# A two-layer hybrid attention trunk: the first eight loads of modulation weights shared between two issuing queues

## The chip, the cores and the metric

The kernel runs on one core of a Trainium2 chip. The core has a matrix engine (PE, with its weight loads listed apart as PEld), a vector engine (DVE), a scalar engine (ACT), GpSimd (POOL) and a sync engine (SP) that here only issues transfers. The metric is the device time of one execution in microseconds (us); lower is better. For the kernel before the change, three runs gave a median of 1925.78 us (1925.18 to 1926.59).

## What is computed

The input x has 512 rows and 2048 columns. Two layers are computed, all in float32; what matters here is how each layer begins:

```python
c_act = jax.nn.silu(c)                               # c: 2048 numbers
mod = c_act @ w_mod[l] + b_mod[l]                    # w_mod[l]: 2048 x 6144
shift, scale, gate = jnp.split(mod, 3, axis=-1)
h = x * (1.0 + scale[:, None]) + shift[:, None]
proj = h @ w_in                                      # layer 0: 2048 x 8192, then attention
...
x = layer_norm(DN_ALPHA * x + gate[:, None] * y, ln_g[l], ln_b[l])
```

Layer 0 is differential attention with 8 heads, layer 1 forgetting attention with 16 heads on keys and values projected once. Nothing of `h` exists before its columns of `shift` and `scale` do, and each of these needs a whole column of `w_mod`, 2048 rows deep.

## The kernel before, in words

Each float32 product is made of three products of rounded parts (high with high, high with low, low with high), so weights and activations are split: ACT casts the high part (`whi` at L125, `hh` at L694), DVE subtracts to get the low part (`wlo` at L132, `hl` at L709).

The start of the kernel makes `h` in the order of its 16 column blocks ("kt") while the first projections of two heads already run. The 16 blocks are grouped in nine sets, of which the first two hold one block each. For set 0, the weights of shift and scale are 2048 rows by 128 columns, twice: 2 MB. They come as eight loads of 256 KB, named **load 0 to load 7** below: loads 0 to 3 fill one tile (`sms_121` before, `sms_109` after the change), rows 0 to 1023, loads 4 to 7 the next tile (`sms_126`), rows 1024 to 2047; an even number is shift, an odd one scale, and each pair brings 512 rows. Loads 8 and on belong to set 1.

What is done with them: DVE multiplies 128 rows at a time by the column of `cact` that belongs to them and adds up in `sacc` (L616 for the first rows, L618 for the rest). Rows 6, 9, 10 and 13 (in blocks of 128) are left to PE (L646). Rows 12, 14 and 15 of the DVE's share, and row 13 of PE's, need loads 6 and 7. PE then sums `sacc` over the partitions (L660), DVE adds the bias and stores into `mcol` (L671), and only then can ACT make `hh` of block 0 (L694) and `htmp` (L701), from which DVE makes `hl` (L709). PE's projections of block 0 (L720) follow.

The order of each engine in this start is written out by hand as strings of letters (`ORDER_SP`, `ORDER_ACT`, `ORDER_PE`, `ORDER_DVE`): `L` is a load of modulation weights, `X` a load of x, `W` a load of projection weights (two transfers each), `a` a cast, `b` its subtraction, `F` a multiplication of PE that fills time and whose result nobody reads (L632), and so on. Before the strings are played, the kernel loads `c` and a part of the bias (L235, L236) on SP's queue and works out `cact = silu(c)` from it (L241 to L247). All loads of the start stand in SP's queue.

Every transfer counts its landing on one of eight completion counters, `DMAHW0` to `DMAHW7`, handed out in turn. A transfer that is given a counter for the second or third time is issued only after the transfer before it on that counter has landed; the issuing engine waits for it, in order, with all that stands behind.

Of the kernel before, what the change touches and what calls it, by code (L numbers as in the profile page):

```python
# [13 lines left out]
AF = mybir.ActivationFunctionType  # L14
ALU = mybir.AluOpType

P = 128
D = 2048
KT = D // P
# [125 lines left out]
def tile_yoco(  # L145
# [23 lines left out]
    nc = tc.nc  # L169
    V, S, PE, G = nc.vector, nc.scalar, nc.tensor, nc.gpsimd  # L170
# [25 lines left out]
    def tr_bank(name="tr"):  # L196
        return ps.tile([P, 512], F32, name=name, tag="tr", bufs=1)
# [14 lines left out]
    def corner(sc, q, k):  # L212
# [6 lines left out]
    ident = const.tile([P, P], F32, name="ident")  # L219
# [3 lines left out]
    mask = const.tile([P, 512], F32, name="mask")  # L223
# [7 lines left out]
    crow, brow = (  # L231
        kpool.tile([P, T], F32, name=name, tag="K")[:k, 0:P]
        for name, k in (("crow", KT), ("brow", 32))
    )
    nc.sync.dma_start(crow, c[0].rearrange("(a p) -> a p", p=P))  # L235
    nc.sync.dma_start(brow, b_mod[0, 0 : 2 * D].rearrange("(a p) -> a p", p=P))  # L236
    ccol = const.tile([P, KT], F32, name="ccol")
    pcol = const.tile([P, 38], F32, name="pcol")
    bcol = const.tile([P, 2, KT], F32, name="bcol")
    pt = tr_bank()  # L240
    PE.transpose(pt[:, 0:KT], crow, ident[0:KT, 0:KT])  # L241
    V.tensor_copy(ccol, pt[:, 0:KT])
    cact = const.tile([P, KT], F32, name="cact")
    tc.keep_in_program_order(S.activation(cact, ccol, AF.Exp, scale=-1.0))
    V.tensor_scalar(cact, cact, 1.0, None, op0=ALU.add)
    V.reciprocal(cact, cact)
    V.tensor_tensor(cact, cact, ccol, op=ALU.mult)  # L247
    pt = tr_bank()
    PE.transpose(pt[:, 0:32], brow, ident[0:32, 0:32])
    V.tensor_copy(bcol[:, 0, :], pt[:, 0:16])  # L250
    V.tensor_scalar(bcol[:, 1, :], pt[:, 16:32], 1.0, None, op0=ALU.add)
    gcol, bncol = pcol[:, 0:16], pcol[:, 16:32]

    neglam = const.tile([P, 1], F32, name="neglam")
# [232 lines left out]
    with tc.tile_pool(name="start", bufs=2, reuse_waits="tile") as sp, tc.manual_schedule(engines=MANUAL):  # L487
        mcol = const.tile([P, 2, KT], F32, name="mcol")

        fill = kpool.tile([P, T], F32R, name="fill", tag="K")  # L490
        S.copy(fill[:, 0:384], mask[:, 0:384])
        tiles = []
        for i, (k0, nk) in enumerate(sets):
            nr = 8 // nk
# [41 lines left out]
        cnt = dict.fromkeys("LXWpdmlbahicretoABCF", 0)  # L536
# [4 lines left out]
        def rows_read(n):  # L541

            i, k, nr = tiles[n]
            return all(
                ((i, r) in e_list[: cnt["e"]] if r in rows_pe[i] else (i, r) in d_list[: cnt["d"]]) for r in range(k, k + nr)
            )
# [12 lines left out]
        def op_L(j, queue=None):  # L559
            n, kq, step, v = loads[j]  # L560
            i, k, nr = tiles[n]
            k0, nk = sets[i]
            if n not in mtile:
                if n >= NBUF and not rows_read(n - NBUF):
                    return False
                mtile[n] = sp.tile([P, nr, 2, nk * P], F32, name="sms", tag="sms", bufs=NBUF)
            rows = w_mod[0, (k + kq) * P : (k + kq + step) * P, v * D + k0 * P : v * D + (k0 + nk) * P]
            (queue or nc.sync).dma_start(mtile[n][:, kq : kq + step, v, :], rows.rearrange("(k p) n -> p k n", p=P))  # L568
            return True
# [214 lines left out]
        def written(text):  # L784

            out, n = [], ""
            for ch in text:
                if ch.isdigit():
                    n += ch
                elif not ch.isspace():  # L790
                    out += (list("ABC") if ch == "g" else [ch]) * int(n or 1)
                    n = ""
            return out

        lists = [written(text) for text in (ORDER_SP, ORDER_ACT, ORDER_PE, ORDER_DVE)]
        kinds = ("LXWp", "ahicrK", "etoABCF", "dmlb")
        for text, kind in zip(lists, kinds):
            for ch in kind:
                if ch not in "KF":
                    text += [ch] * (total[ch] - text.count(ch) - (text.count("K") if ch == "L" else 0) - (lists[1].count("K") if ch == "L" else 0))  # L800
        at = [0] * 4
        while any(a < len(t) for a, t in zip(at, lists)):
            moved = False
# [1038 lines left out]
```

## Time and profile before

| what | value |
|---|---|
| median of three runs | 1925.78 us |
| the profiled execution, its own time | 1927.05 us |
| its span, first to last instruction | 1925.3 us |
| PE busy | 1910.1 us, 99% of the span |
| DVE, ACT busy | 1371.0 us, 732.9 us |
| mean granted clock of PE | 0.999 |
| moved by DMA | 382.22 MB, mean 199 GB/s |

Times below count from the first instruction of the profiled execution. In a row of the timeline stand the start, the time from the first start to the last end of the merged instructions, engine and line, what is written and read, how many, and in brackets the idle time of that engine before it and what ended it. "SPq" is SP's queue: the time in which it issues a transfer, not the one in which the data moves. An overlapped matmul is listed longer than the distance to the next one.

### The profile page before, as it was taken

Reading aid. Unit: us, or ns where it says so; the run is one execution under the profiler, and the core shown is the slowest. Engines: PE = TensorE matmul, PEld = TensorE weight load, DVE = VectorE, ACT = ScalarE, POOL = GpSimd, SP = SyncE. Lnnn points to the kernel's source line nnn. Section 1 sums busy time; section 2 is a strip of 40 time slices with the busy share of each in tenths; the row PEclk is TensorE's granted clock in tenths of the full one; section 3 lists DMA queues with packets and bytes.
Section 4 is the critical chain, followed back from the end, with each engine's and each line's share of the span. In section 5 each row is a group of like instructions: output and inputs, shape, how many; then the busy total and the mean of one; then the engine's idle time right before and its main releaser. Section 6 shows DMA issues by size and latency. Waiting matters only on the chain.

```text
span 1925.3 us, 25879 instructions
## 1 busy us (share of the span) xinstructions
PE 1910.1 (99%) x8921; PEld 1593.8 (83%) x8921; DVE 1371.0 (71%) x2617; ACT 732.9 (38%) x1266; POOL 2.3 (0%) x11
## 2 busy tenths in 40 slices
PE   8999999999999999999999999999999999999998
PEld 6888888888888888888888898888888888888887
DVE  7994588777776768667675477777566666686768
ACT  3656344333332344521272232224344344453122
POOL 0000000000000000000000000000000000000000
PEclk9999999999999999999999999999999999999999
DMA  9993566676767676476547586775345555555622
GB/s 339 385 339 91 158 187 197 209 239 189 235 197 225 203 225 182 123 241 221 184 164 251 181 297 209 250 266 162 112 147 159 158 150 162 154 153 168 226 93 110
DMA packets 352275, 382.22 MB, mean 199 GB/s; under 512 B 77912, under 2 KB 256244, under 8 KB 351376
## 3 DMA queue, kind: packets, MB, share of 16 engines
q1 hardware_dynamic: 349120, 376.25, 61.7%
q10 hardware_dynamic: 3024, 4.33, 0.6%
q8 instruction: 70, 1.15, 0.2%
q14 instruction: 61, 0.50, 0.1%
HBM read 348.68 MB, written 31.80 MB: 198 GB/s over the span
## 4 chain that ended last, share of the span: by engine, by line
PE 96%; DVE 2%; SPq 1%; DMA 1%; issue 0%; ACT 0%; DVEq 0%; ACTq 0%
PE acc L208 26%; PE acc L209 26%; PE acc L210 26%; PE acc L720 4%; PE sc L720 2%; PE sc L210 1%; PE sc L209 1%; PE sc L208 1%; PE o L208 1%; PE o L210 1%; PE o L209 1%; PE o L720 1%; SPq L568 1%; DMA sms<-in_w_mod_dram 0%; PE tr L686 0%
## 5 line engine op out<-in xcount | busy, mean ns | idle before, releaser
L113 ACT CAST whi<-wst 128x1024 fp32r<-128x1024 f32 (+2 forms) x298 | 303.4, 1018 | 616.4 <-PE acc L210 314.1
L114 DVE TENSOR_TENSOR wlo<-wst,whi 128x1024 fp32r<-128x1024 f32 (+2 forms) x298 | 351.4, 1180 | 248.5 <-ACT whi L113 222.7
L208 PE MATMUL acc<-hh,whi 128*128 128x512 f32 x1184 | 463.2, 391 | 0.0
L209 PE MATMUL acc<-hl,whi 128*128 128x512 f32 x1184 | 462.0, 390 | 0.0
L210 PE MATMUL acc<-hh,wlo 128*128 128x512 f32 x1184 | 460.3, 390 | 0.0
L208 PE MATMUL acc<-whi,hh 128*128 128x512 f32 (+1 forms) x1104 | 418.8, 380 | 0.0
L209 PE MATMUL acc<-wlo,hh 128*128 128x512 f32 (+1 forms) x1104 | 417.0, 378 | 0.0
L210 PE MATMUL acc<-whi,hl 128*128 128x512 f32 (+1 forms) x1104 | 416.5, 378 | 0.0
L433 DVE SCALAR_TENSOR_TENSOR macc<-ms,cact,macc 128x512 f32<-128x512 f32 x307 | 228.9, 746 | 61.2 <-DMA ms<-in_w_mod_dram 44.4
L210 PEld LDWEIGHTS acc<-hh,wlo 128*128 128x128 f32 x1184 | 222.4, 188 | 47.0
L208 PEld LDWEIGHTS acc<-hh,whi 128*128 128x128 f32 x1184 | 222.5, 188 | 44.1 <-DVE sgb L1509 0.8
L209 PEld LDWEIGHTS acc<-hl,whi 128*128 128x128 f32 x1184 | 222.6, 188 | 42.2
L210 PEld LDWEIGHTS acc<-whi,hl 128*128 128x128 f32 x1104 | 207.4, 188 | 38.6
L208 PEld LDWEIGHTS acc<-whi,hh 128*128 128x128 f32 x1104 | 207.4, 188 | 37.5 <-DVE ztmp L1241 0.6
L209 PEld LDWEIGHTS acc<-wlo,hh 128*128 128x128 f32 x1104 | 207.5, 188 | 35.6
L618 DVE SCALAR_TENSOR_TENSOR sacc<-sms,cact,sacc 128x512 f32<-128x512 f32 (+1 forms) x128 | 89.9, 702 | 6.2 <-DMA sms<-in_w_mod_dram 2.9
L904 ACT ACTIVATE e<-e,mn 128x128 f32<-128x128 f32 (+3 forms) x64 | 36.0, 563 | 111.1 <-DVE mn L900 104.5
L1559 ACT ACTIVATE eb<-eb,mnb 128x128 f32<-128x128 f32 (+1 forms) x64 | 35.9, 561 | 73.8 <-DVE mnb L1556 73.5
L720 PE MATMUL acc<-wlo,hh 128*128 128x512 f32 x128 | 49.9, 399 | 0.6 <-DVE wlo L132 0.6
L720 PE MATMUL acc<-whi,hl 128*128 128x512 f32 x128 | 49.4, 394 | 0.0
L720 PE MATMUL acc<-whi,hh 128*128 128x512 f32 x128 | 49.2, 393 | 0.0
L132 DVE TENSOR_TENSOR wlo<-wst,whi 128x768 fp32r<-128x768 f32 (+1 forms) x32 | 34.8, 1088 | 17.3 <-ACT whi L125 16.2
(336 smaller groups left out, 2095.6 us busy)
## 6 DMA issues: line engine op xcount, KB each, us to landing
wst<-in_a_w_in_dram SPq DMA_DIRECT2D x240, 256.0 KB
ms<-in_w_mod_dram SPq DMA_DIRECT2D x136, 256.0 KB
ms<-in_kv_w_mod_dram SPq DMA_DIRECT2D x64, 512.0 KB
wst<-in_b_w_in_dram SPq DMA_DIRECT2D x128, 256.0 KB
sms<-in_w_mod_dram SPq DMA_DIRECT2D x56, 512.0 KB
wst<-in_kv_w_dram SPq DMA_DIRECT2D x56, 512.0 KB
ms<-in_w_mod_dram SPq DMA_DIRECT2D x32, 512.0 KB
wst<-in_a_w_out_dram SPq DMA_DIRECT2D x32, 512.0 KB
```

The costliest lines, as they stand in the source:

```text
L113: self.nc.scalar.copy(hi[:, :, :w], st[:, :, :w])
L114: self.nc.vector.tensor_tensor(lo[:, :, :w], st[:, :, :w], hi[:, :, :w].bitcast(F32), op=ALU.subtract)
L132: self.nc.vector.tensor_tensor(lo[:, :, :w], st[:, :, :w], hi[:, :, :w].bitcast(F32), op=ALU.subtract)
L208: PE.matmul(dst, lhs[0], rhs[0], start=start, stop=False, skip_group_check=True)
L209: PE.matmul(dst, lhs[0], rhs[1], start=False, stop=False, skip_group_check=True)
L210: PE.matmul(dst, lhs[1], rhs[0], start=False, stop=stop, skip_group_check=True)
L433: ins = V.scalar_tensor_tensor(acc, w, cact[:, kt : kt + 1], acc, op0=ALU.mult, op1=ALU.add)
L568: (queue or nc.sync).dma_start(mtile[n][:, kq : kq + step, v, :], rows.rearrange("(k p) n -> p k n", p=P))
L618: V.scalar_tensor_tensor(acc, w, sc, acc, op0=ALU.mult, op1=ALU.add)
L720: PE.matmul(bank[n, bk], l, r, start=start, stop=stop, skip_group_check=True)
L904: S.activation(e[:, :w], e[:, :w], AF.Exp, bias=mn, scale=-1.0, accum_out=rs)
L1559: S.activation(e[:, :w], e[:, :w], AF.Exp, bias=mn, scale=-1.0, accum_out=rs)
```

## The change

The loads of `c` and of the bias, the work on `cact`, and the cast that makes the operand of PE's fillers move from the head of the kernel to the place just before the strings are played, and the first eight `L` are taken out of the strings and issued by hand, four of them on ACT's queue:

```diff
+        def first_loads(*queues):
+            for queue in queues:
+                op_L(cnt["L"], queue)
+                cnt["L"] += 1
+                del lists[0][lists[0].index("L")]
+
+        nc.sync.dma_start(crow, c[0].rearrange("(a p) -> a p", p=P))
+        nc.sync.dma_start(brow, b_mod[0, 0 : 2 * D].rearrange("(a p) -> a p", p=P))
+        first_loads(nc.scalar, nc.sync, nc.scalar, nc.sync)
+        pt = tr_bank()
+        PE.transpose(pt[:, 0:KT], crow, ident[0:KT, 0:KT])
+        V.tensor_copy(ccol, pt[:, 0:KT])
+        S.activation(cact, ccol, AF.Exp, scale=-1.0)
...
+        S.copy(fill[:, 0:384], mask[:, 0:384])
+        first_loads(nc.sync, nc.scalar, nc.sync, nc.scalar)
```

So ACT issues loads 0, 2, 5 and 7, SP loads 1, 3, 4 and 6. Outside these places and the first six rows of DVE (the two that make `bcol` now stand behind the three that make `cact`) every engine has the same instructions in the same order as before.

The first rows of ACT before; a DMA row is a transfer that the engine issues, "waits" names the counters that it must see first:

```order
L244 ACT_TABLE_LOAD
L244 ACTIVATE cact_101<-ccol_95 128x16 [waits DVE_49]
L491 CAST fill_119<-mask_86 128x384 [waits Pool_49]
L125 CAST whi_153<-wst_136 128x2x384 [waits DMAHW6_49,DMAHW5_49]
L694 ACTIVATE hh_214<-px_168,mcol_118 128x512 [waits DVE_49]
```

The first rows of ACT in the change:

```order
L554 DMA sms_109<-in_w_mod_dram 128x4x128 x2
L799 ACT_TABLE_LOAD
L799 ACTIVATE cact_96<-ccol_93 128x16 [waits DVE_49]
L807 CAST fill_106<-mask_86 128x384 [waits Pool_49]
L554 DMA sms_126<-in_w_mod_dram 128x4x128 [waits DMAHW0_49]
L554 DMA sms_126<-in_w_mod_dram 128x4x128 [waits DMAHW2_49]
L125 CAST whi_153<-wst_136 128x2x384 [waits DMAHW4_49,DMAHW3_49]
L680 ACTIVATE hh_214<-px_168,mcol_105 128x512 [waits DVE_49]
```

Loads 0 and 2 now stand ahead of ACT's table load and wait for nothing; loads 5 and 7 stand ahead of its first cast and wait for a counter each.

The first rows of SP before (the first four loads, then loads 4 and 5, then 6 and 7 each with a counter, x, and set 1 with the first projection weights):

```order
L235 DMA crow_91<-in_c_dram 16x128
L236 DMA brow_92<-in_b_mod_dram 32x128
L568 DMA sms_121<-in_w_mod_dram 128x4x128 x4
L568 DMA sms_126<-in_w_mod_dram 128x4x128 x2
L568 DMA sms_126<-in_w_mod_dram 128x4x128 [waits DMAHW0_49]
L568 DMA sms_126<-in_w_mod_dram 128x4x128 [waits DMAHW1_49]
L578 DMA xt_131<-in_x_dram 128x4x128 [waits DMAHW2_49]
L568 DMA sms_133<-in_w_mod_dram 128x4x128 [waits DMAHW3_49]
L568 DMA sms_133<-in_w_mod_dram 128x4x128 [waits DMAHW4_49]
L63 DMA wst_136<-in_a_w_in_dram 128x2x256 [waits DMAHW5_49]
```

The first rows of SP in the change (loads 1 and 3, then 4 and 6, then x and what follows):

```order
L793 DMA crow_91<-in_c_dram 16x128
L794 DMA brow_92<-in_b_mod_dram 32x128
L554 DMA sms_109<-in_w_mod_dram 128x4x128 x2
L554 DMA sms_126<-in_w_mod_dram 128x4x128 x2
L564 DMA xt_131<-in_x_dram 128x4x128 [waits DMAHW0_49]
L554 DMA sms_133<-in_w_mod_dram 128x4x128 [waits DMAHW1_49]
L554 DMA sms_133<-in_w_mod_dram 128x4x128 [waits DMAHW2_49]
L63 DMA wst_136<-in_a_w_in_dram 128x2x256 [waits DMAHW3_49]
L63 DMA wst_136<-in_a_w_in_dram 128x2x128 [waits DMAHW4_49]
L554 DMA sms_133<-in_w_mod_dram 128x4x128 [waits DMAHW5_49]
L63 DMA wst_140<-in_a_w_in_dram 128x2x256 [waits DMAHW6_49]
L63 DMA wst_140<-in_a_w_in_dram 128x2x256 [waits DMAHW7_49]
```

SP issues four transfers fewer ahead of x. Counter by counter, the built program hands out: 0 to load 0, then x, then load 5; 1 to `c`, load 8, load 11; 2 to the bias, load 9, load 7; 3 to load 2 and 4 to load 1, then each to half of the first projection weights. Each landing adds 16. The wait of load 5 is for 32 on counter 0, which is the landing of x; that of load 7 is for 32 on counter 2, which is the landing of load 9.

More of the change, by code (lines that the diff above doesn't have):

```diff
@@ L234, in tile_yoco @@
     )
-    nc.sync.dma_start(crow, c[0].rearrange("(a p) -> a p", p=P))
-    nc.sync.dma_start(brow, b_mod[0, 0 : 2 * D].rearrange("(a p) -> a p", p=P))
     ccol = const.tile([P, KT], F32, name="ccol")
@@ L239, in tile_yoco @@
     bcol = const.tile([P, 2, KT], F32, name="bcol")
-    pt = tr_bank()
-    PE.transpose(pt[:, 0:KT], crow, ident[0:KT, 0:KT])
-    V.tensor_copy(ccol, pt[:, 0:KT])
     cact = const.tile([P, KT], F32, name="cact")
[L244 to L251, printed above, removed]
     gcol, bncol = pcol[:, 0:16], pcol[:, 16:32]
@@ L490, in tile_yoco @@
         fill = kpool.tile([P, T], F32R, name="fill", tag="K")
-        S.copy(fill[:, 0:384], mask[:, 0:384])
         tiles = []
@@ L800, in tile_yoco @@
                     text += [ch] * (total[ch] - text.count(ch) - (text.count("K") if ch == "L" else 0) - (lists[1].count("K") if ch == "L" else 0))
+        def first_loads(*queues):
[10 more added lines that the diff above has]
+        S.activation(cact, ccol, AF.Exp, scale=-1.0)
+        V.tensor_scalar(cact, cact, 1.0, None, op0=ALU.add)
+        V.reciprocal(cact, cact)
+        V.tensor_tensor(cact, cact, ccol, op=ALU.mult)
+        pt = tr_bank()
+        PE.transpose(pt[:, 0:32], brow, ident[0:32, 0:32])
+        V.tensor_copy(bcol[:, 0, :], pt[:, 0:16])
+        V.tensor_scalar(bcol[:, 1, :], pt[:, 16:32], 1.0, None, op0=ALU.add)
+        S.copy(fill[:, 0:384], mask[:, 0:384])
+        first_loads(nc.sync, nc.scalar, nc.sync, nc.scalar)
         at = [0] * 4
```

## The prediction

> **What bounds the kernel now.** I read the page's first line and its table of engines, then the chain of work that ended last.
>
> ```profile
> span 1925.3 us, 25879 instructions
> PE 1910.1 (99%) x8921; PEld 1593.8 (83%) x8921; DVE 1371.0 (71%) x2617; ACT 732.9 (38%) x1266; POOL 2.3 (0%) x11
> PE 96%; DVE 2%; SPq 1%; DMA 1%; issue 0%; ACT 0%; DVEq 0%; ACTq 0%
> ```
>
> PE carries 96% of the chain. The rest, some 4%, lies mostly ahead of PE's steady work. A change to the first eight loads can therefore move the end only by moving the moment at which PE stops waiting. So the next view is PE's timeline over the first 60 us, for the rows where PE waited after its first projection.
>
> ```profile
> 15.97 0.73 PE L720 MATMUL sc<-hh,whi 128*128 128x512 f32 x2
> 17.37 0.73 PE L720 MATMUL sc<-hl,whi 128*128 128x512 f32 x2 [0.43 <-DVE hl L709]
> 25.39 0.73 PE L720 MATMUL sc<-hh,whi 128*128 128x512 f32 x2 [0.87 <-ACT hh L694]
> 36.03 0.74 PE L720 MATMUL acc<-wlo,hh 128*128 128x512 f32 x2 [0.60 <-DVE wlo L132]
> 60.00:120.00 60.00, 60.00 (x291) 49.97 (x290) 55.20 (x77) 37.35 (x56) 0.00 (x0) 1.00 1.05 364
> ```
>
> Projections begin at 15.97; PE then waits three times, 0.43 + 0.87 + 0.60 = 1.90 us in all, and from 36.03 on it does not wait again in this stage (the last row is the window from 60 to 120 us, whose second number is PE's busy time: all of it). A delay that reaches PE before 36.03 is passed to the end, less what these waits can swallow. What the start itself waits for:
>
> ```profile
> 0.73 0.40 SPq L235 DMA_DIRECT2D crow<-in_c_dram  x1
> 1.64 5.58 SPq L568 DMA_DIRECT2D sms<-in_w_mod_dram  x8
> 7.26 0.69 SPq L578 DMA_DIRECT2D xt<-in_x_dram  x1
> 2.58 0.26 PE L241 MATMUL tr<-ident,crow 16*128 16x16 f32 x1 [2.58 <-DMA crow<-in_c_dram]
> 5.30 0.35 DVE L616 TENSOR_SCALAR sacc<-sms,cact 128x256 f32<-128x256 f32 x1 [1.01 <-DMA sms<-in_w_mod_dram]
> 11.10 1.52 DVE L618 SCALAR_TENSOR_TENSOR sacc<-sms,cact,sacc 128x256 f32<-128x256 f32 x3 [0.48 <-DMA sms<-in_w_mod_dram]
> 13.00 0.85 PE L660 MATMUL tr<-ones,sacc 128*128 128x1 f32 x4
> 13.37 0.35 DVE L616 TENSOR_SCALAR sacc<-sms,cact 128x256 f32<-128x256 f32 x1 [0.74 <-DMA sms<-in_w_mod_dram]
> 13.72 2.38 PE L632 MATMUL fb<-fill 128*128 128x384 f32 x7
> 13.89 0.16 DVE L671 TENSOR_TENSOR mcol<-tr,bcol 128x2 f32<-128x2 f32 x1 [0.17 <-PE tr L660]
> 14.41 0.83 ACT L125 CAST whi<-wst 128x768 fp32r<-128x768 f32 x1 [10.71 <-DMA wst<-in_a_w_in_dram]
> 15.14 0.77 ACT L694 ACTIVATE hh<-px,mcol 128x512 fp32r<-128x512 f32 x1
> ```
>
> DVE's three waits are landings: loads 0 and 1 by 5.30, loads 6 and 7 by 11.10, loads 8 and 9 by 13.37. ACT's is the first projection weights, by 14.41. From loads 6 and 7 the path runs on through L618, L660, L671 and ACT's L694; PE meanwhile runs its seven fillers, which end when `hh` is there. The start is a queue of transfers, so I also read how full the DMA engines are (last number GB/s, the one before it their busy share).
>
> ```profile
> 0.00:4.00 4.00, 0.72 (x3) 0.54 (x4) 0.69 (x5) 1.90 (x3) 1.60 (x9) 1.00 0.27 77
> 4.50:6.50 2.00, 0.00 (x0) 0.00 (x0) 1.13 (x3) 0.00 (x0) 0.00 (x0) 1.00 0.84 224
> 10.00:12.00 2.00, 2.00 (x10) 2.00 (x11) 1.44 (x4) 0.00 (x0) 0.00 (x0) 1.00 1.14 342
> ```
>
> At 342 GB/s a load of 262 kB takes 0.77 us; x, load 8 and load 9, the three that land from 11.10 to 13.37, give 2.27 / 3 = 0.76. The engines are full by 10 us and were not from 4.5 to 6.5.
>
> **What the change removes and adds.** *Issue moved forward.* The first load was issued at 1.64, behind `c` and the bias; on ACT's queue it can be issued at 0.73, 0.91 us earlier. Loads 5 and 7 also leave the queue ahead of x, so x is the seventh large transfer and not the ninth: 2 x 0.76 = 1.52 earlier. Before, x landed one transfer behind load 7: 11.10 + 0.76 = 11.86. In the change: 11.86 - 0.91 - 1.52 = **9.43**. Load 9 follows two transfers later, at 10.95.
>
> *Waits added.* By the rows of ACT and their counters, load 5 is issued only when x has landed and load 7 only when load 9 has landed. That turns round the order in which data is needed: set 1's load 9 comes ahead of set 0's load 7. Load 7 is issued at about 10.95 + 0.10 = 11.05. Its own way has two terms: `c`, a load of 8 kB, was issued at 0.73 and released PE at 2.58, so 1.85 us pass apart from the moving of data, and the data takes 0.77 at full rate. 11.05 + 1.85 + 0.77 = **13.67**, where load 7 had landed by 11.10. Call the difference s = 13.67 - 11.10 = 2.57 us.
>
> No row here shows a load of ACT's queue beside a full queue of SP's, so its price is bounded from both sides. At the least, the transfers run without the slack of 4.5 to 6.5: at 224 GB/s, 2 x (1 - 224/342) = 0.69 us could come back and s be 1.88. At the most it waits like a load behind SP's own backlog: x was issued at 7.26 and landed at 11.86, 4.60 later; 11.05 + 4.60 = 15.65, s = 4.55. I take 2.57, near the lower end, because ACT's own queue is empty then and the row of `c` is the one of an empty queue.
>
> [...]
>
> *What s does further on.* The last three rows of DVE's set 0 start at 13.67, and L660, L671 follow as before: `mcol` at 13.89 + 2.57 = 16.46. The fillers of PE stand behind L660 in PE's order, so PE's first projection is at 15.97 + 2.57 = 18.54. DVE's low part comes from this row, with an idle time before it that a later start removes:
>
> ```profile
> 16.62 0.69 DVE L709 TENSOR_TENSOR hl<-htmp,hh 128x512 fp32r<-128x512 f32 x1 [0.26 <-ACT htmp L701]
> 18.83 4.12 DVE L618 SCALAR_TENSOR_TENSOR sacc<-sms,cact,sacc 128x256 f32<-128x256 f32 x8
> 23.65 0.16 DVE L671 TENSOR_TENSOR mcol<-tr,bcol 128x2 f32<-128x2 f32 x1
> 31.72 3.11 DVE L618 SCALAR_TENSOR_TENSOR sacc<-sms,cact,sacc 128x512 f32<-128x512 f32 x4 [1.22 <-DMA sms<-in_w_mod_dram]
> ```
>
> So `hl` is late by 2.57 - 0.26 = 2.31. From there through `mcol` of set 1 at 23.65 DVE has next to no idle time, so PE's row at 25.39 is late by 2.31 too. Up to 36.03 two things swallow: PE's own wait of 0.60, and DVE's 1.22 for a landing at 31.72, which is no longer waited for as the transfers are early. The larger remainder counts: PE 2.31 - 0.60 = 1.71, DVE 2.31 - 1.22 = 1.09. **The sum is +1.71 us**, or s - 0.86.
>
> *Edits at nothing.* The table load moves behind two issues of some 0.45 us each, to about 1.6, and its activation waits for `ccol` anyway:
>
> ```profile
> 0.73 1.28 ACT L244 ACT_TABLE_LOAD   x1 [0.73 <-PEq L1829]
> 3.08 0.21 ACT L244 ACTIVATE cact<-ccol 128x16 f32<-128x16 f32 x1 [1.07 <-DVE ccol L242]
> ```
>
> 1.07 us idle covers 0.9 of delay; beyond that DVE's 1.01 at 5.30 covers. `c` and the bias now travel beside loads 0 and 2. If they are held up by both, 2 x 0.77 = 1.54, DVE starts set 0 that much later, at 6.8; it has nine rows of some 0.5 us there before its last three, 4.6 us, and until 13.67 to do them, so nothing comes of it. Two `bcol` rows of 0.17 us behind `cact` lie in the same idle time. On ACT, the first cast stands behind the issue of load 7 (over by about 11.6); its weights, before at 14.41, come 0.91 + 1.52 earlier, near 12, and `hh` waits for `mcol` at 16.46, which covers it by over 3 us. If load 9 were late by more than that, the cast and with it `hh`, `htmp` and every later cast would be.
>
> **Rivals.** *The change does what it says: early loads, early start.* Then the wait of ACT costs nothing and the 0.91 us (with the 0.69 of slack, 1.60) arrive at PE: the start at 15.06 to 14.37. Later waits take part of it, since transfers are early by the same: -0.9, up to -1.6. For it: 77 GB/s in the first 4 us, room that a second queue can fill. Against: it needs load 7 by 10.2, and x alone, the seventh transfer, cannot land before 0.73 + 1.85 + 7 x 0.77 = 7.97, load 9 not before 9.5, load 7 not before 9.5 + 2.7 = 12.2 (s = 1.1, +0.2).
>
> *Load 7 behind SP's backlog.* One mechanism: the DMA engines serve ACT's late loads as if they stood at the end of SP's queue. Place: load 7, 4.60 us from issue to landing; price s = 4.55, +3.7 us. [...] For it: the engines' share of 1.14 at 10 to 12 us, no gap to slip into. Against: ACT's queue is empty.
>
> *Washed out.* If transfers gain more by 25 us than I count, or s is the 1.1 above, PE is at 36.03 within 0.3 us of before: 0. For: only s beyond 0.86 arrives. Against: DVE has next to nothing to give between 16.6 and 30.5 us:
>
> ```profile
> 16.60:30.50 13.90, 12.60 (x64) 9.98 (x63) 13.28 (x22) 4.64 (x7) 0.00 (x0) 1.00 1.11 373
> ```
>
> Its fourth number is DVE's busy time, 13.28 of 13.90, and the rest is in gaps between instructions.
>
> **How the numbers follow.** The profiled execution took 1927.05 us with a span of 1925.3, so 1.75 lie around it; it stands 1.27 above the median of the runs, 1925.78. Against its own time the forecast is 1927.05 + 1.7 = 1928.8, and against the median 1925.78 + 1.7 = **1927.5**. Chances: forecast 0.60 (+0.6 to +2.8 by the bounds and the half rate), backlog 0.14 (+3.7, 1929.5), washed out 0.14 (1925.8), early start 0.12 (-0.9 to -1.6, 1924.2 to 1924.9). The three runs before differ by 1.4 us, so I allow 0.3 beyond the backlog's time: 1924.6 to 1929.8.
>
> A measurement of this kernel can tell about 0.2% from no change, which is 3.9 us. Of the cases only the far end of the backlog gets there: slower 0.05. A gain of 3.9 us would need more than the start holds: 0.01. Within 0.2%: 0.94.
>
> **What would show it.** Right: ACT's third and fourth transfers issued near 9.5 and 11; DVE idle for some 2 to 3 us ahead of its last three rows of set 0, which start near 13.7; L671 near 16.5; PE's first projection near 18.5; no wait at the row that stood at 36.03, and that row 1.7 us later. Wrong: ACT's late issues before 8 us, or those three DVE rows before 12, for the early start; the three rows after 15, for the backlog. Also wrong would be a PE that waits again after 36 us, where I count nothing: the weights of the next steps then come later than PE needs them.

## The result, and the profile after

The changed kernel takes 1931.30 us (median of nine runs, 1930.53 to 1932.17); the kernel before took 1926.22 in the nine runs beside them (1925.18 to 1927.72). The ratio is 1.0025, interval 1.0016 to 1.0034: **slower by 5.1 us, 0.26%**. The forecast was +1.7, and its range ended at 1929.8. The profiled execution took 1931.31 with a span of 1929.5.

The page of the changed kernel, with the same three lines as shown of before:

```profile
span 1929.5 us, 25877 instructions
PE 1910.2 (99%) x8921; PEld 1594.0 (83%) x8921; DVE 1370.4 (71%) x2617; ACT 732.6 (38%) x1266; POOL 2.3 (0%) x11
PE 97%; DVE 1%; DMA 1%; SPq 0%; issue 0%; ACT 0%; ACTq 0%
```

PE is busy for 1910.2 us, where it was 1910.1. So the span's 4.2 us more are time in which PE has nothing to do. (The profiled execution of before, 1927.05, stood 0.83 above the median of the nine runs, that of the change at its own; 4.26 + 0.83 = 5.09, the difference of the medians.)

The chain of waits of the changed kernel over the start, in order of time (start, us, what; a DMA row runs from the issue to the landing, "..." stands for rows left out, and rows named issue, of 0.04 at most, are left out without it):

```profile
0.73 2.99 DMA sms<-in_w_mod_dram
3.76 1.55 SPq L564
5.35 0.77 SPq L554
6.17 4.39 DMA sms<-in_w_mod_dram
10.58 5.82 DMA sms<-in_w_mod_dram
16.45 0.58 PE tr L632 x2
...
19.08 2.45 PE fb L618 x7
21.53 0.85 PE sc L706 x2
...
24.53 0.46 PE acc L706 x2
```

This view shows where the time goes. Load 0 lands at 3.72; that lets SP issue x (3.76, L564), then loads 8 and 9. Load 9 is issued at 6.17 and lands at 10.56, which lets ACT issue load 7 at 10.58, and load 7 is 5.82 us on its way. PE goes on 0.05 after it has landed. The row at 19.08 is PE's seven fillers: `hh` is there from 20.09 on (19.31 + 0.78 on ACT), but the fillers stand ahead of the first projection in PE's order and hold it until 21.33; no run left them out. Two rows are for later: two projections of one size take 0.85 at 21.53 and 0.46 at 24.53.

The timeline of the changed kernel (start, us, engine, line, operation, in brackets the idle time before and what ended it):

```profile
6.12 0.35 DVE L602 TENSOR_SCALAR sacc<-sms,cact 128x256 f32<-128x256 f32 x1 [1.47 <-DMA sms<-in_w_mod_dram]
9.10 1.86 ACTq L554 DMA_DIRECT2D sms<-in_w_mod_dram  x2
11.73 0.83 ACT L125 CAST whi<-wst 128x768 fp32r<-128x768 f32 x1 [7.55 <-DMA wst<-in_a_w_in_dram]
14.44 2.59 PE L632 MATMUL tr<-cact,sms 128*128 128x1 f32 x10 [6.29 <-DMA sms<-in_w_mod_dram]
14.48 1.01 DVE L604 SCALAR_TENSOR_TENSOR sacc<-sms,cact,sacc 128x256 f32<-128x256 f32 x2 [4.88 <-DMA sms<-in_w_mod_dram]
16.48 1.53 DVE L604 SCALAR_TENSOR_TENSOR sacc<-sms,cact,sacc 128x256 f32<-128x256 f32 x3 [1.00 <-DMA sms<-in_w_mod_dram]
19.12 0.16 DVE L657 TENSOR_TENSOR mcol<-tr,bcol 128x2 f32<-128x2 f32 x1 [0.84 <-PE tr L646]
19.31 0.78 ACT L680 ACTIVATE hh<-px,mcol 128x512 fp32r<-128x512 f32 x1 [6.75 <-DVE mcol L657]
21.33 1.05 PE L706 MATMUL sc<-hh,whi 128*128 128x512 f32 x2
28.48 0.50 PE L646 MATMUL tr<-ones,sacc 128*128 128x1 f32 x4
29.02 0.16 DVE L657 TENSOR_TENSOR mcol<-tr,bcol 128x2 f32<-128x2 f32 x1 [0.87 <-PE tr L646]
30.77 0.73 PE L706 MATMUL sc<-hh,whi 128*128 128x512 f32 x2 [0.87 <-ACT hh L680]
40.65 0.61 PE L706 MATMUL acc<-wlo,hh 128*128 128x512 f32 x2
```

DVE's last three rows of set 0 stand at 16.48, where they were at 11.10: **s is 5.38**. Row by row the lateness of PE is: first projection 15.97 to 21.33, +5.36; second block 25.39 to 30.77, +5.38; the row that stood at 36.03 with a wait of 0.60 is at 40.65 with none, +4.62; the span, +4.2. The casts were in time (11.73, long before `mcol` at 19.12).

Three windows of the changed kernel (from:to, length, busy PE, PEld, DVE, ACT, POOL, granted clock, DMA share, GB/s):

```profile
11.50:16.50 5.00, 1.92 (x9) 1.84 (x9) 0.99 (x3) 0.83 (x1) 0.00 (x0) 1.00 1.14 353
21.30:23.60 2.30, 2.30 (x7) 1.78 (x7) 2.30 (x4) 0.40 (x1) 0.00 (x0) 1.00 1.10 382
60.00:120.00 60.00, 60.00 (x295) 50.03 (x295) 55.04 (x77) 37.87 (x58) 0.00 (x0) 1.00 0.99 334
```

While PE and DVE wait for load 7, the DMA engines run at 353 GB/s. Most of what they move is other data: by the counters further below, what was issued before load 7. From 60 us on PE is busy all the time, as before.

### The profile page after: what moved, and what is told of

It is laid out like the page before. It is cut to its first block, busy times and chain, and to the rows that moved or that the text cites. A ratio compares the mean times of both kernels' runs of the same rounds, so it can differ in the third digit from the quotient of the medians.

```text
span 1929.5 us, 25877 instructions
## 1 busy us (share of the span) xinstructions
PE 1910.2 (99%) x8921; PEld 1594.0 (83%) x8921; DVE 1370.4 (71%) x2617; ACT 732.6 (38%) x1266; POOL 2.3 (0%) x11
## 3 DMA queue, kind: packets, MB, share of 16 engines
q10 hardware_dynamic: 5136, 5.38, 0.8%
## 4 chain that ended last, share of the span: by engine, by line
PE 97%; DVE 1%; DMA 1%; SPq 0%; issue 0%; ACT 0%; ACTq 0%
PE acc L208 26%; PE acc L209 26%; PE acc L210 26%; PE acc L706 5%; PE sc L706 2%; PE sc L210 1%; PE sc L209 1%; PE sc L208 1%; PE o L208 1%; PE o L210 1%; PE o L706 1%; PE o L209 1%; DMA sms<-in_w_mod_dram 1%; PE tr L646 0%; PE tr L672 0%; DMA ms<-in_w_mod_dram 0%
## 5 line engine op out<-in xcount | busy, mean ns | idle before, releaser
L113 ACT CAST whi<-wst 128x1024 fp32r<-128x1024 f32 (+2 forms) x298 | 303.4, 1018 | 618.4 <-PE acc L210 300.9
L604 DVE SCALAR_TENSOR_TENSOR sacc<-sms,cact,sacc 128x512 f32<-128x512 f32 (+1 forms) x128 | 89.9, 703 | 10.2 <-DMA sms<-in_w_mod_dram 6.8
```

Source lines behind the costliest of these rows:

```text
L113: self.nc.scalar.copy(hi[:, :, :w], st[:, :, :w])
L604: V.scalar_tensor_tensor(acc, w, sc, acc, op0=ALU.mult, op1=ALU.add)
```

## The experiments

**Which half loses: two kernels.** `first_loads` shares the first four loads, then the next four. One kernel keeps the early sharing only (ACT has loads 0 and 2, nothing later), the other the late sharing only (ACT has loads 5 and 7).

Early half alone:

```diff
         S.copy(fill[:, 0:384], mask[:, 0:384])
-        first_loads(nc.sync, nc.scalar, nc.sync, nc.scalar)
+        first_loads(nc.sync, nc.sync, nc.sync, nc.sync)
```

> Only the early half of the change: ACT issues loads 0 and 2 ahead of its table load, loads 5 and 7 stay on SP's queue in their places. Theory (the loss comes from loads 5 and 7 being issued only after x and load 9 have landed): the loss is gone; eight loads land by about 9.8 us, the last three DVE rows of set 0 start near 9.9 (11.10 before), PE's first projection near 14.8 (15.97 before), time -0.3 to -1.2 us against before. Rival (two issuing queues cost by themselves, in c arriving later or in shared DMA engines): +1 us or more, with DVE's last three rows at 11 or later.

Measured: 1925.43 us (11 runs, 1924.67 to 1926.80) against 1926.58 of before (31 runs); ratio 0.9994, interval 0.9985 to 1.0003. The timeline of this kernel:

```profile
6.20 5.69 DVE L604 SCALAR_TENSOR_TENSOR sacc<-sms,cact,sacc 128x256 f32<-128x256 f32 x11
15.21 1.05 PE L706 MATMUL sc<-hh,whi 128*128 128x512 f32 x2
16.49 1.05 PE L706 MATMUL sc<-hl,whi 128*128 128x512 f32 x2
25.11 0.73 PE L706 MATMUL sc<-hh,whi 128*128 128x512 f32 x2 [0.87 <-ACT hh L680]
```

DVE's eleven rows of L604 run without a wait: load 7 is no longer the last thing. PE starts 0.76 earlier than before (15.21 against 15.97), of which 0.28 is left at the second block (25.11 against 25.39), since its first projections run at a slow rate (1.05 a pair; more on this below). Before, PE then had the wait of 0.60 at 36.03, which is gone here: matched row by row, PE is 1.0 ahead there and 1.5 from 60 us on. Nothing of the loss is in this half.

Late half alone:

```diff
         nc.sync.dma_start(brow, b_mod[0, 0 : 2 * D].rearrange("(a p) -> a p", p=P))
-        first_loads(nc.scalar, nc.sync, nc.scalar, nc.sync)
+        first_loads(nc.sync, nc.sync, nc.sync, nc.sync)
```

> Only the late half of the change: loads 0 to 4 and 6 on SP, loads 5 and 7 on ACT behind the cast of the filler, so that they wait for the landing of load 4 and of x. Theory with in-order service (a late load lands behind all that SP issued before it, 5.3 to 5.8 us from issue to landing as in the change): load 7 issued near 10.3, lands near 15.9, time +3.5 to +5 us. Rival (ACT's queue gets a share of its own, 2.6 to 3.4 us from issue to landing): lands near 13.3, time +1.5 to +2.5 us.

Measured: 1931.39 us (8 runs, 1930.51 to 1932.47); ratio 1.0026, interval 1.0016 to 1.0036. Its chain of waits, and then its timeline:

```profile
5.24 4.81 DMA xt<-in_x_dram
10.07 6.39 DMA sms<-in_w_mod_dram
```

```profile
8.55 1.91 ACTq L554 DMA_DIRECT2D sms<-in_w_mod_dram  x2
16.54 1.53 DVE L604 SCALAR_TENSOR_TENSOR sacc<-sms,cact,sacc 128x256 f32<-128x256 f32 x3 [1.35 <-DMA sms<-in_w_mod_dram]
```

The whole loss is here: the same time as the change, the three rows at 16.54, load 7 issued at 10.07 and 6.39 us on its way, longer than the 5.3 to 5.8 expected.

**Is it ACT's queue or the late issue?** In this kernel ACT still issues loads 0, 2, 5 and 7, but all of them ahead of its table load, so loads 5 and 7 wait for no counter.

```diff
         first_loads(nc.scalar, nc.sync, nc.scalar, nc.sync)
+        first_loads(nc.sync, nc.scalar, nc.sync, nc.scalar)
         pt = tr_bank()
...
         S.copy(fill[:, 0:384], mask[:, 0:384])
-        first_loads(nc.sync, nc.scalar, nc.sync, nc.scalar)
```

> The same four loads on ACT, all of them ahead of its table load, so that none waits for a counter on ACT. Theory (lateness of issue is the cause): as the early half alone, DVE's last three rows of set 0 near 10, time -0.2 to -1.2 us against before. Rival (loads 5 and 7 on ACT's queue are slow wherever they are issued): those rows at 13 or later, time +2 us or more.

Measured: 1926.58 us (11 runs, 1925.11 to 1928.82); ratio 1.0001, interval 0.9992 to 1.0010. The chain of this kernel, and then its timeline:

```profile
0.73 3.10 DMA sms<-in_w_mod_dram
3.83 0.02 issue
3.84 6.12 DMA sms<-in_w_mod_dram
```

```profile
8.87 4.13 DVE L604 SCALAR_TENSOR_TENSOR sacc<-sms,cact,sacc 128x256 f32<-128x256 f32 x8 [0.24 <-DMA sms<-in_w_mod_dram]
16.78 0.63 PE L706 MATMUL sc<-hh,whi 128*128 128x512 f32 x2
```

The loss is gone with the same two loads on the same queue: the late issue is its cause, and not ACT's queue as such. By the counters their way is no shorter here (6.43 and 6.89), but they are issued at 1.76 and 2.32 and so land at 8.19 and 9.21. The expected gain did not come: DVE's last three rows start at 11.47 and not near 10. Load 4, now SP's third, waits for the landing of load 0 (3.83) and is 6.12 on its way, behind ACT's four; PE starts at 16.78, 0.8 later than before.

**Does load 7 wait for SP's transfers, or is a late load of ACT slow by itself?** This kernel holds SP's queue: right behind load 9 SP stores 16 rows of load 7 to a scratch tensor that nobody reads, so SP issues nothing more until load 7 has landed. Its time holds that stall of SP, so I read the trace and not the time.

```diff
+        held = dram.tile([16, 4, P], F32, name="held_dram")
...
             (queue or nc.sync).dma_start(mtile[n][:, kq : kq + step, v, :], rows.rearrange("(k p) n -> p k n", p=P))
+            if j == 9:
+                nc.sync.dma_start(held, mtile[1][0:16, 4:8, 1, :])
             return True
```

> The change, with SP's queue emptied behind load 9: SP stores a piece of load 7's data (16 rows of 2 KB) to a scratch tensor before it issues anything more, so it waits for load 7. By the order of the counters ACT now issues loads 5 and 7 when loads 2 and 1 have landed, near 5.9 and 6.5, behind x, load 8 and load 9 but with nothing after them. Theory (one order of service for both queues, by time of issue): load 7 lands last, near 12.1, and DVE's last three rows of set 0 start near 12.2, 5.6 us after the issue. Rival (ACT's queue has a share of its own): load 7 lands near 10, 3.5 us after its issue. The time is worse than before by 1 to 3 us either way, since SP's queue runs dry.

Measured: 1930.87 us in one run, against 1926.52 of before; the 4.35 more are above the 1 to 3 expected. Its chain, and then its timeline:

```profile
5.75 5.81 DMA sms<-in_w_mod_dram
```

```profile
4.69 1.50 ACTq L555 DMA_DIRECT2D sms<-in_w_mod_dram  x2
11.64 1.52 DVE L607 SCALAR_TENSOR_TENSOR sacc<-sms,cact,sacc 128x256 f32<-128x256 f32 x3 [0.55 <-DMA sms<-in_w_mod_dram]
```

Load 7 is issued at 5.75, a little earlier than expected, and only load 9 is issued behind it (at 5.85, landed at 12.58). It still takes 5.81 us, near the 5.6 of service in the order of issue and not the 3.5 of a share of its own; the rows stand at 11.64. So in this kernel what was issued ahead decides, and not what comes behind. The price with little else on the way is in the counters: when SP goes on here, its first load of 256 KB is issued at 12.31 and has landed at 15.31, 3.0 later. ACT's queue was hardly slower: load 0, issued by ACT at the head of the changed kernel, took 2.99, and 2.80 from SP before.

The counters of the transfers give the order itself. This table is worked out from the counter events in the trace of the changed kernel: each landing adds sixteen, "first" is the first of these, "landed" the last. W0 and W1 are the projection weights that come first and second, each in two parts; load 12 is a load of set 1 like load 11.

```
            queue  issued  first   landed  way
W1, part 1  SP       8.66  11.87   13.05   4.38
load 5      ACT      9.10  12.65   14.40   5.30
W1, part 2  SP       9.21  13.32   14.58   5.36
load 11     SP       9.84  14.08   15.57   5.73
load 7      ACT     10.58  14.83   16.40   5.82
load 12     SP      11.23  15.60   16.77   5.54
```

In this table the first parts arrive in the order of issue, 0.67 to 0.78 us apart, whichever engine issued: ACT's load 7 gets its turn between the two transfers of SP that were issued before and after it. The large transfers of the late half alone (but for two issued 0.01 apart), and of the kernel with ACT's four at the head, come in this order too; in the latter loads 5, 7 and 4, issued at 1.76, 2.32 and 3.84, land at 8.19, 9.21 and 9.96. In the kernel that holds SP it is the order in which the issues end, not start (x, from 3.77 on, needs 1.3 us to be issued there, and load 5, from 4.69 on, passes it): load 5, x, load 8, load 7 (landed at 11.56), load 9 (12.58).

**How much of the loss is PE's slow rate?** In the changed kernel two projections take 0.85 us at 21.53 in the chain and 0.46 at 24.53: they follow each other 0.43 apart at first, and 0.23 later. This kernel gives PE 18 more fillers, whose result nobody reads, ahead of its wait for load 5. (REST is the unchanged rest of the string.)

```diff
-ORDER_PE = '4eFto7F' + REST
+ORDER_PE = 'e18F3eFto7F' + REST
```

> The change with 18 more fillers on PE behind its first two row-6 products, where PE otherwise stands idle from 8.2 to 14.4 us. Theory (a part of the loss is PE's slow first projections after that idle time, 0.42 us apart in place of 0.23): the first nine projections keep 0.23 us, PE's row L646 of set 1 comes 0.5 to 0.8 us earlier than the 28.48 of the change, time 0.4 to 0.8 us below the change's 1931.3, about +4.5 against before. Rival (all of the loss is load 7's landing): the time of the change, +5.1.

Measured: 1930.58 us (10 runs, 1929.85 to 1931.17); ratio 1.0021, interval 1.0012 to 1.0031. Its timeline:

```profile
7.08 5.81 PE L618 MATMUL fb<-fill 128*128 128x384 f32 x18
14.32 1.05 PE L632 MATMUL tr<-cact,sms 128*128 128x1 f32 x8 [1.32 <-DMA sms<-in_w_mod_dram]
21.20 1.05 PE L706 MATMUL sc<-hh,whi 128*128 128x512 f32 x2
22.48 0.70 PE L706 MATMUL sc<-hl,whi 128*128 128x512 f32 x2
28.07 0.50 PE L646 MATMUL tr<-ones,sacc 128*128 128x1 f32 x4
```

The pair at 21.20 is as slow as in the change (1.05), the pair at 22.48 nearly fast (0.70; the same pair in the change took 1.01). PE's L646 of set 1 stands at 28.07, 0.41 earlier than in the change, where 0.5 to 0.8 was expected. The median is 0.7 lower than that of the change, but the intervals overlap, so the time alone does not show it. What this kernel takes away of the slow rate is worth some tenths of the 5.1 us; the first three projections are as slow as before, so what all of it costs is not shown. I had thought that the fillers would keep all the first projections fast; they did not, with two waits behind them, the longer of 1.32.

**Does the same hold back the early half?** The early half alone, with seven more fillers of PE, four ahead of its rows of set 0 and three between them:

```diff
-ORDER_PE = '4eFto7F' + REST
+ORDER_PE = '4FeFeFeFeFto7F' + REST
...
-        first_loads(nc.sync, nc.scalar, nc.sync, nc.scalar)
+        first_loads(nc.sync, nc.sync, nc.sync, nc.sync)
```

> The early half alone, with eight fillers of PE moved in front of and between its products of set 0, so that PE works from 5.4 us on. Theory (the early half's start is held by PE, whose first projections run at half speed until 18.2 us): projections at 0.23 us from the first on, PE's L646 of set 1 by 22.4 (22.84 in the early half), time 0.3 to 1 us below the early half's 1925.4. Rival (DVE and transfers hold it): the same time as the early half.

Measured: 1925.99 us (11 runs, 1924.91 to 1927.94) against 1926.52 (21 runs); ratio 0.9998, interval 0.9989 to 1.0007. Its timeline:

```profile
15.07 1.05 PE L706 MATMUL sc<-hh,whi 128*128 128x512 f32 x2
24.00 0.74 PE L706 MATMUL sc<-hh,whi 128*128 128x512 f32 x2 [0.87 <-ACT hh L680]
33.92 0.72 PE L706 MATMUL acc<-wlo,hh 128*128 128x512 f32 x2
986.95 0.66 PE L1348 MATMUL sc<-ident,n 128*128 128x128 f32 x4 [0.42 <-DVE n L1361]
```

The first pair of projections is still slow (1.05), where all were expected to be fast. PE is at the second block 1.1 us earlier than in the early half without the fillers (24.00 against 25.11), and at the row of 36.03 it is 2.1 ahead of before, where the early half is 1.0 ahead. The time has none of it. My theory, that this is what keeps the gain small, fell. In the profiled execution part of it is given back in layer 1: matched row by row, PE is 2.55 ahead of before at 340 us and 1.67 ahead at 1018, with a new wait for DVE at 986.95. One execution shows that; whether it is so in all of them stays open.

**Is ACT's queue needed for the gain?** All eight loads on SP's queue, which starts with them; `c` and the bias go to ACT's.

```diff
-        nc.sync.dma_start(crow, c[0].rearrange("(a p) -> a p", p=P))
-        nc.sync.dma_start(brow, b_mod[0, 0 : 2 * D].rearrange("(a p) -> a p", p=P))
-        first_loads(nc.scalar, nc.sync, nc.scalar, nc.sync)
+        nc.scalar.dma_start(crow, c[0].rearrange("(a p) -> a p", p=P))
+        nc.scalar.dma_start(brow, b_mod[0, 0 : 2 * D].rearrange("(a p) -> a p", p=P))
+        first_loads(nc.sync, nc.sync, nc.sync, nc.sync)
...
-        first_loads(nc.sync, nc.scalar, nc.sync, nc.scalar)
+        first_loads(nc.sync, nc.sync, nc.sync, nc.sync)
```

> The other way round: c and the bias on ACT's queue ahead of its table load, all eight loads on SP, so that load 0 is issued at 0.73 too and no load is late. Theory (what the early half gains is the 0.91 us of issue): load 7 lands near 10, PE's first projection near 15, time -0.5 to -1.5 us against before, as the early half (1925.4). Rival (the gain needs large loads from two queues): the time of before within 0.3 us.

Measured: 1925.58 us (11 runs, 1924.59 to 1927.47); ratio 0.9995, interval 0.9987 to 1.0004. Its timeline:

```profile
10.32 1.53 DVE L604 SCALAR_TENSOR_TENSOR sacc<-sms,cact,sacc 128x256 f32<-128x256 f32 x3 [0.47 <-DMA sms<-in_w_mod_dram]
15.54 1.22 PE L706 MATMUL sc<-hh,whi 128*128 128x512 f32 x2
```

The three rows stand 0.78 earlier than before (10.32 against 11.10), PE's start 0.43. The time is that of the early half: about 1 us less than before, which the interval does not separate from none. So the times show no need of a large load on a second queue. The traces are less even: by the counters load 7 lands at 10.98 before, at 10.19 here and at 9.68 in the early half, and matched row by row PE is 0.8 ahead of before at 60 us here and 1.5 in the early half. Whether two queues bring this half microsecond in every execution stays open, with one profile of each.

## Why the prediction was wrong, step by step

**The step that failed** is the way of load 7: "Its own way has two terms: `c` [...] 1.85 us pass apart from the moving of data, and the data takes 0.77 at full rate", 2.62 in all, taken "because ACT's own queue is empty then". It measured 5.82. Nor was the queue empty: by the prediction's own terms load 5, issued at 9.43, lands at 12.05, after load 7 is issued at 11.05, and in the trace it was on its way from 9.10 to 14.40. Load 5 is the one that met an empty ACT queue (load 2 had landed at 5.81), and it took 5.30. The second queue gave load 7 no second place in the service: the table shows turns in the order of issue across both, 0.67 to 0.78 us apart. That was the rival "load 7 behind SP's backlog", which got a chance of 0.14; the sign named for it, those three rows after 15, is there (16.48).

**The bound was too small as well.** I took 4.60, the way of x before, as the most. By the counters, five transfers were issued and not landed when x was issued before: with x itself six, 6 x 0.76 = 4.6. When load 7 is issued at 10.58 there are seven such: both parts of W0 (the second half as large), load 10, W1 in two parts, load 5 and load 11. With load 7 itself that is 7.5 x 0.76 = 5.7, an estimate from the transfer time in the prediction, against 5.82 measured. Counted in the same way, load 11 and load 12 of the table come to 5.7 too (5.73 and 5.54 measured), load 5 to 4.9 (5.30), and load 7 of the late half alone to 5.7 (6.39), so the estimate can be short by 0.7. What the prediction did not count is what stands issued and not landed ahead of load 7, load 5 of the same queue included.

No run shows the half rate that the forecast's range counts with, that is a load of ACT at half the speed beside SP's full queue, nor the 3.4 us of the rival in the late half's expectation, which was my estimate for that from the prediction's terms (1.85 + 2 x 0.77): load 5, which met an empty ACT queue, took 5.30. The times, too, show nothing that a second issuing queue would add: 1925.58 us for the kernel with all eight loads on SP's queue, 1925.43 for the early half.

**Right: when load 7 is issued.** Load 5 was forecast at 9.43 and issued at 9.10, load 7 at 11.05 and issued at 10.58. The counters set this order as read from the program.

**Right in size: what comes after s.** s - 0.86 with s = 5.38 is 4.52; PE's row of 36.03 is 4.62 later and the span 4.2. Term by term it came otherwise, so that the sum fits is in part luck. The 0.60 at 36.03 went, as forecast. The 0.26 ahead of `hl` came back at that row (no wait, 16.62 to 21.50, +4.88), but was lost again by the second block (+5.38). The start of set 1's sum on PE, before:

```profile
23.00 0.61 PE L660 MATMUL tr<-ones,sacc 128*128 128x1 f32 x4
```

From the first projection to this row PE needed 23.00 - 15.97 = 7.03 us, 0.43 of it a wait; in the change 28.48 - 21.33 = 7.15 and no wait. The 0.55 more are PE's slow rate, which the prediction did not price, and DVE waits for it (0.87 at 29.02). I had put that rate down to the 6.29 us of idle time, but this is not shown: in the early half alone PE has no wait over 0.88 us from 5 us on, and its first eight projections come 0.43 apart as well. Before, PE's fillers were slow too (0.32 apart) and the rate rose at 15.5, just ahead of the first projection; in the change it rose at 23.5, behind the first five. A further 0.4 of the lateness was gone by the row that stood at 39.24; from there to the end it stays between 4.2 and 4.4.

That a part of s costs nothing has its reason in the chain of the kernel before. Up to 36.03 it does not pass load 7 but runs along SP's queue to a load that is issued at 23.16 and that DVE waits for at 31.72:

```profile
23.16 8.45 DMA sms<-in_w_mod_dram
```

**Two readings that were off.** The prediction says that the 4% of the chain that is not PE lies mostly ahead of PE's steady work; worked out from the chain, it is 35 of 78 us, and the rest lies near 330, near 970 and at the end. The lateness passes those unchanged within 0.2, so nothing followed from it. And the forecast's case is given as +0.6 to +2.8, while its own lower bound, s = 1.88, comes to +1.0 by s - 0.86, and its upper one, s = 4.55, to the +3.7 of the backlog.

**Right: the edits at nothing.** The late table load delays no row that counts, the weights of the first cast were there in time. For the early loads, the sharing gave none of the 0.91 to DVE's first row, which stands at 6.12 and stood at 5.30. By the counters load 0 lands 0.7 earlier than before (3.72), but ACT's load 2 goes ahead of SP's load 1, which is needed first and lands at 5.99, before at 5.17.

**The chances.** The likeliest case was chosen by the row nearest in kind (an empty queue) and not by the one nearest in load (engines full at 1.14). Slower by over 0.2% had 0.05, since the far end of the backlog was thought to be 4.55.

## What to carry to other kernels

Where the DMA engines are as full as here (1.14 busy, 353 GB/s), price a transfer on an idle queue by what all queues have issued and not landed, times the time of one transfer: that estimate gives 5.7 us for load 7, measured at 5.82 in the change and 6.39 in the late half alone, and an empty queue did not shorten the way of the load that met it (5.30). Before a load is moved to another engine, read which counter it must wait for: counters handed out in turn can tie it to the landing of a transfer that is needed later than itself, as load 7 was tied to load 9 (landed at 10.56). Share loads between queues in the order of need, the pair that is needed first ahead of all others: here load 1, behind ACT's load 2, landed at 5.99, before at 5.17.

## What the runs showed of the hardware

In the changed kernel the transfers of ACT and SP that stand in the table were served in one order of issue: first parts 0.67 to 0.78 us apart, ACT's ones among SP's, at 353 GB/s from 11.5 to 16.5 us. In these rows ACT's spread more in landing, 1.57 and 1.75 us from first to last part, while SP's took 1.17 to 1.49; in the kernel with ACT's four at the head, SP's load 4 took 1.98 as well.

In the changed kernel PE's first projections came 0.43 us apart, later ones 0.23, while the granted clock in the row of the window 21.30 to 23.60 reads 1.00. So this column does not show that slowness here. What sets the rate is not shown. In the kernel with 18 fillers, 5.81 us of work ahead of two waits, the longer of 1.32 us, did not keep PE at the fast rate: its products of one column came 0.11 apart between these waits (0.21 to 0.23 in the change, from 14.44 on), and the fillers behind the second 0.32 apart, as in the change.
